# Summing the first modulation vectors over rows on VectorE instead of the matrix engine, in a two-block transformer kernel

## The chip, the core and the metric

The kernel runs on one core of a Trainium2 chip. A core has engines with a queue of instructions each: TensorE (PE, matrix multiply; its weight loads are listed as PEld), VectorE (DVE), ScalarE (ACT), GpSimd (POOL) and SyncE (SP), which here issues the DMAs. The metric is the device time of one execution in microseconds; lower is better.

## The reference, cut to what matters

Two blocks run one after the other on x of 256 rows by 1024 columns, all in fp32. The first is a mixer of four branches, a layer norm, a mixture of 16 experts and a second layer norm. The second is two layers of three sublayers; each sublayer is modulated by vectors made from a condition c:

```python
cond = jax.nn.silu(c)                       # 1024 numbers
for i in range(DEPTH_2):                    # 2 layers
    mod = cond @ ada_w[i] + ada_b[i]        # 1024 x 9216 weights per layer
    sh0, sc0, g0, sh1, sc1, g1, sh2, sc2, g2 = jnp.split(mod, N_MOD, axis=-1)
    h = modulate(rmsnorm(x, pre_norm[i, 0]), sh0, sc0)
    ...
```

The change is about sh0, sc0 and g0 of layer 0, three vectors of 1024 numbers: each is cond times a 1024 x 1024 block of ada_w. They depend on c alone and can be made at any time before the second block; the kernel makes them in the mixer.

## The kernel before

**Weights.** All weights come as slabs of 1 MB in the order of a plan (class `Weights`). A slab lands in a raw buffer (`raw`, three of them in the mixer; later also `rex`, `wex`, `wey`, `wez`, `wea` and `b4`, which the trace calls b). A slab of kind "split" is then split for the matmuls into a high and a low part: ScalarE writes `whi` (L125) and VectorE `wlo` (L126), in 8 pieces of 128x256. A projection does three matmuls per piece (L276 to L278: high by high, low by high, high by low). `pump` issues the next transfer when a buffer comes free, and splits one slab ahead.

**Modulation.** A slab of kind "ada" holds 256 rows of a block of `ada_w` (two chunks of 128 rows, 1024 columns). Twelve of them make the three vectors of layer 0, sublayer 0: four per vector. The plan interleaves them with the mixer's weights. When the plan comes to one, `side` (L2117) is called. For these twelve the flag `vec` is off: `rowsum` (L2146) multiplies each chunk by its column of cond on TensorE, four matmuls of 128x256 that write rows 0, 32, 64 and 96 of one PSUM tile (`adacc`) over eight chunks. With `vec` on, as for most later vectors, VectorE keeps a running sum `asum` of 128x1024 (L2138 for the first chunk, L2140 for the other seven), and only at the end a `rowsum` with a column of ones sums it over the 128 partitions.

**Draining.** When the next "ada" slab comes, or at the mixer's end, `drain` (L2151) copies `adacc` to `aev` (VectorE, L2160) and writes it out in four small DMAs to `arow` (L2163). `finish` (L2166) adds the bias (`ab`, L2173) later.

**The mixer.** Its projections (`psmm`) fill TensorE's queue. Between them lie the serial parts of the branches: the triangular solve of the delta rule, with `TT` and `mt` on VectorE and `psgdn` and `psgla` on TensorE (L767 to L779), the stick-breaking attention, the gated linear attention, and the merges (`mg`, `macc`, L1103 to L1106). At its end `macc` is split to `xTh` and `xTl` and the output projection (`y`) begins in PSUM banks that the mixer has held until then. The experts' matmuls are `pg`, `pu` and `pd` (L1395).

**Order.** The code is written in the order of the computation. A scheduler sets the order in each engine's queue from the dependences, the buffers and this order; `behind` only says that an instruction comes after given ones. Queues run in order.

Of the kernel before, what the change touches and what calls it, by code (L numbers as in the profile page):

```python
# [198 lines left out]
def interleave(main, side, a, b):  # L199
    out, n = [], 0  # L200
    for i, m in enumerate(main):
        out.append(m)
        while n < len(side) and i + 1 > a + (b - a) * n / len(side):
            out.append(side[n])
            n += 1
    return out + side[n:]
# [251 lines left out]
def mixer_slabs(w_in, w_branch, w_out):  # L458
    w = w_in
    out = []  # L460
    def seg(a, b):
        for c in range(a, b, 256):
            out.append(cols_slab(w, c, c + 256))
    seg(1024, 1536)
    kind, parts, n, c = out[0]
    (_, src), = parts
    out[0] = kind, [((h, h + 4, 0, c), src[:, h:h + 4]) for h in (0, 4)], n, c
    out.append(("split", [((0, KC, 0, 16), w.rearrange("(k p) n -> p k n", p=P)[:, :, 5640:5656]),
                          ((0, KC, 16, 24), w.rearrange("(k p) n -> p k n", p=P)[:, :, 2048:2056])], KC, 24))
    for nm, s in FILL:  # L470
        c = {"q": 512, "v": 1536, "s": 2568}[nm] + 256 * s
        seg(c, c + 256)
    merge = lambda n: mslabs(w, w_branch, n)
    seg(3592, 4104)
    seg(0, 512)
    out += merge(2) + merge(0)
    seg(4616, 5128)
    seg(4104, 4616)
    seg(5128, 5640)
    seg(2056, 2568)  # L480
    out += merge(1)
    seg(5656, 6168)
    out += merge(3)
    for r in range(0, D, 256):
        out.append(rows_slab(w_out, r, r + 256))
    return out
# [712 lines left out]
def moe_slabs(wg, wu, wd):  # L1199
    out = []  # L1200
    raw = lambda w, r: ("raw",) + rows_slab(w, r, r + 1 * RB * P)[1:]
    for q in range(0, E, 2):
        for r in range(0, D, RB * P):
            for w in (wg, wu):
                out += [raw(w[e], r) for e in (q, q + 1)]
        for r in range(0, FE, 2 * P):
            out += [("raw",) + rows_slab(wd[e], r, r + 2 * P)[1:] for e in (q, q + 1)]
    return out


def router_consts(k, a):
    nc, cp = k.nc, k.consts
    wr = cp.tile([P, KC, 2 * E], F32, name="wr")
    nc.gpsimd.memset(wr, 0.0)
    nc.sync.dma_start(out=wr[:, :, 0:E], in_=a["w_router"].rearrange("(k p) e -> p k e", p=P))
    rb = cp.tile([P, 1, E], F32, name="rb")
    nc.sync.dma_start(out=rb[:, 0], in_=bcast(a["router_bias"], E))
    it = cp.tile([P, CAP], F32, name="it")
    nc.gpsimd.iota(it, pattern=[[1, CAP]], base=0, channel_multiplier=0, allow_small_or_imprecise_dtypes=True)
    k.router = wr, rb, it  # L1220


def router_bias(k, bcol, psum_tile):
    nc = k.nc
    pb = psum_tile([P, E])
    for kc in range(KC):
        nc.tensor.matmul(pb, bcol[:, kc:kc + 1].to_broadcast([P, P]), k.router[0][:, kc, 0:E], start=kc == 0, stop=kc == KC - 1)
    k.lnw = k.consts.tile([P, E], F32, name="lnw")
    nc.vector.tensor_copy(k.lnw, pb)
# [511 lines left out]
def load_pos(k, pool, positions):  # L1741
    nc = k.nc
    pi = pool.tile([P, 2], I32, name="rp_i")
    v = bass.AP(tensor=positions.tensor, offset=positions.offset, ap=[[1, P], [P, 2]])
    if positions.dtype == I32:
        nc.sync.dma_start(out=pi, in_=v)
    else:
        p64 = pool.tile([P, 2], positions.dtype, name="rp_64")
        nc.sync.dma_start(out=p64, in_=v)
        nc.vector.tensor_copy(pi, p64.bitcast(I32).rearrange("p (t w) -> p t w", w=2)[:, :, 0])  # L1750
    return pi
# [559 lines left out]
def tile_kernel(ctx, tc, a, out):  # L2311
    nc = tc.nc
    e = ctx.enter_context
    k = Kern(tc)
# [7 lines left out]
    A = k.A = Ada(k, a)  # L2322
    k.W.side = A.side
    k.ops = Ops(nc, tc, k.consts, k.small)
    ms = mixer_slabs(a["w_in"][0], a["w_branch"][0], a["w_out"][0])
    k.W.plan(interleave(ms[:-4], A.slabs(0, 0, False), 4, len(ms) - 6) + ms[-4:])
    k.W.plan(moe_slabs(a["w_gate"][0], a["w_up"][0], a["w_down"][0]))
    k.W.plan(second_slabs(a, A))
    new_x = lambda: k.act.tile([P, 2, D], F32, name="x", tag="x", bufs=1)
# [21 lines left out]

    k.more_slots = more_slots
    with ExitStack() as c:
        m = Mixer(k, c, a, x, xTh, xTl)
        A.setup(adp, dram, lambda s: m.ps.tile(s, F32, name="adps", tag="gdn", bufs=2))
        A.acc_tile(m.ps.tile([P, 512], F32, name="adacc", tag="adacc", bufs=1))
        pos = []

        def later():
            pos.append(load_pos(k, adp, a["positions_2"]))  # L2360
            A.load(m.bp)
            router_consts(k, a)

        def then():
            A.params()
            router_bias(k, A.ln1b, A.psum_tile)

        m.run(later, then)
        k.W.bufs["b4"] = 4
        k.W.side_some(99)  # L2370
        A.drain()
# [75 lines left out]


# [12 lines left out]
```

## Time and profile before

| | |
|---|---|
| median of 3 runs | 1732.62 us (1730.42 to 1734.5) |
| the profiled execution | 1734.04 us, its span 1732.3 us, mean granted clock 0.989 |
| busy TensorE, VectorE, ScalarE, GpSimd | 1676.4, 1122.9, 836.2, 28.3 us |
| read from HBM | 401.11 MB, 232 GB/s over the span |
| chain that ended last | TensorE 51%, VectorE 6%, ScalarE 2%, DMA 1% |

The mixer lasts to about 415 us, the first layer norm and the router to 456 us, the experts to 686 us; then come the second layer norm and the second block. Times in rows are from the span's start. In a row of the stretches each engine has its busy time and, in brackets, its instructions.

### The profile page before, as it was taken

What the parts mean: (1) busy time and instruction counts of PE and PEld (TensorE: products, weight loads), DVE (VectorE), ACT (ScalarE), POOL (GpSimd) and SP (SyncE); (2) the same over time, 40 slices, a digit from 0 to 9 for tenths busy, and PEclk for the clock granted to TensorE, in tenths of its full rate; (3) what the DMA queues carried; (4) which work ended last, traced back from release to release, by engine and by line L of the source; (5) the groups of instructions that cost most, each with busy time, mean ns of one, the idle gap of its engine ahead of it and who ended that gap; (6) DMA issues with size and microseconds to landing.
All of it is one profiled execution on the core that took longest, in us unless ns stands there. A gap on an engine that the chain in (4) does not pass through costs nothing.

```text
span 1732.3 us, 30933 instructions
## 1 busy us (share of the span) xinstructions
PE 1676.4 (97%) x11786; PEld 1412.0 (82%) x11786; DVE 1122.9 (65%) x3100; ACT 836.2 (48%) x2367; POOL 28.3 (2%) x61
## 2 busy tenths in 40 slices
PE   7999999999899997999999999999999999999998
PEld 6998999998534443899878599988999778889986
DVE  5776676666521112888859788895977576786563
ACT  5446594344211111555644755563655475656552
POOL 1000011010000000000000000000000000000000
PEclk9999999999999999899999999999999999999999
DMA  6334657459999996599834659893988656347550
GB/s 209 122 122 147 194 177 236 149 182 353 353 390 395 395 392 251 174 308 302 318 107 149 245 189 312 288 346 118 325 259 274 223 188 218 130 145 250 174 204 25
DMA packets 247267, 404.35 MB, mean 233 GB/s; under 512 B 16271, under 2 KB 167478, under 8 KB 247110
## 3 DMA queue, kind: packets, MB, share of 16 engines
q1 hardware_dynamic: 247110, 402.29, 67.6%
q8 instruction: 95, 1.56, 0.4%
q14 instruction: 62, 0.51, 0.1%
HBM read 401.11 MB, written 1.07 MB: 232 GB/s over the span
## 4 chain that ended last, share of the span: by engine, by line
PE 51%; DVE 6%; ACT 2%; DMA 1%; issue 1%; DVEq 0%; ACTq 0%
PE y L276 5%; PE y L278 5%; PE y L277 5%; PE psg L276 4%; PE psg L277 4%; PE psg L278 4%; PE psu L276 4%; PE psu L278 4%; PE psu L277 4%; PE y L1596 2%; PE pj L277 1%; PE adacc L2148 1%; PE pj L276 1%; PE pj L278 1%; DVE wlo L126 1%; ACT scr L288 1%
## 5 line engine op out<-in xcount | busy, mean ns | idle before, releaser
L125 ACT ACTIVATE whi<-raw 128x256 fp32r<-128x256 f32 (+1 forms) x1005 | 330.0, 406 | 231.8 <-PE psmm L277 68.0
L126 DVE TENSOR_TENSOR wlo<-raw,whi 128x256 fp32r<-128x256 f32 (+1 forms) x1005 | 368.6, 425 | 103.6 <-ACT whi L125 103.2
L276 PE MATMUL psmm<-xTh,whi 128*128 128x256 f32 x584 | 170.6, 292 | 7.0 <-DVE gdn_k L592 5.1
L277 PE MATMUL psmm<-xTl,whi 128*128 128x256 f32 x584 | 167.6, 287 | 0.0
L278 PE MATMUL psmm<-xTh,wlo 128*128 128x256 f32 x584 | 167.4, 287 | 0.0
L276 PE MATMUL psg<-xTh,whi 128*128 128x256 f32 x560 | 159.0, 284 | 0.0
L278 PE MATMUL psg<-xTh,wlo 128*128 128x256 f32 x560 | 158.4, 283 | 0.0
L277 PE MATMUL psg<-xTl,whi 128*128 128x256 f32 x560 | 158.4, 283 | 0.0
L126 DVE TENSOR_TENSOR wlo<-rex,whi 128x256 fp32r<-128x256 f32 x296 | 104.1, 417 | 28.9 <-ACT whi L125 28.5
L125 ACT ACTIVATE whi<-rex 128x256 fp32r<-128x256 f32 x296 | 97.1, 405 | 52.9 <-PE y L278 15.4
L276 PEld LDWEIGHTS psmm<-xTh,whi 128*128 128x128 f32 x584 | 112.1, 192 | 12.0 <-ACT whi L125 7.2
L278 PEld LDWEIGHTS psmm<-xTh,wlo 128*128 128x128 f32 x584 | 112.1, 192 | 0.6
L277 PEld LDWEIGHTS psmm<-xTl,whi 128*128 128x128 f32 x584 | 112.1, 192 | 0.5
L276 PE MATMUL psu<-xTh,whi 128*128 128x256 f32 x392 | 111.0, 283 | 0.0
L277 PE MATMUL psu<-xTl,whi 128*128 128x256 f32 x392 | 110.9, 283 | 0.0
L278 PE MATMUL psu<-xTh,wlo 128*128 128x256 f32 x392 | 110.9, 283 | 0.0
L276 PEld LDWEIGHTS psg<-xTh,whi 128*128 128x128 f32 x560 | 107.4, 192 | 1.3 <-issue 1.3
L277 PEld LDWEIGHTS psg<-xTl,whi 128*128 128x128 f32 x560 | 107.4, 192 | 0.0
L278 PEld LDWEIGHTS psg<-xTh,wlo 128*128 128x128 f32 x560 | 107.4, 192 | 0.0
L276 PE MATMUL y<-whi,hh 128*128 128x512 f32 x264 | 105.5, 400 | 0.0
L278 PE MATMUL y<-whi,hl 128*128 128x512 f32 x264 | 104.5, 396 | 0.0
L277 PE MATMUL y<-wlo,hh 128*128 128x512 f32 x264 | 104.4, 395 | 0.0
(696 smaller groups left out, 4057.0 us busy)
## 6 DMA issues: line engine op xcount, KB each, us to landing
raw<-in_ada_w_dram SPq DMA_DIRECT2D x60, 1024.0 KB
raw<-in_w_in_dram SPq DMA_DIRECT2D x39, 1024.0 KB
raw<-in_ffn_w_up_dram SPq DMA_DIRECT2D x33, 1024.0 KB
raw<-in_ffn_w_down_dram SPq DMA_DIRECT2D x28, 1024.0 KB
raw<-in_ffn_w_gate_dram SPq DMA_DIRECT2D x27, 1024.0 KB
rex<-in_ffn_w_gate_dram SPq DMA_DIRECT2D x13, 1024.0 KB
rex<-in_ada_w_dram SPq DMA_DIRECT2D x12, 1024.0 KB
rex<-in_ffn_w_down_dram SPq DMA_DIRECT2D x12, 1024.0 KB
```

Source lines behind the costliest of these rows:

```text
L125: nc.scalar.activation(hi[:, c0:c1], t[:, c0:c1], AF.Copy)
L126: nc.vector.tensor_tensor(lo[:, c0:c1], t[:, c0:c1], hi[:, c0:c1].bitcast(F32), op=OP.subtract)
L276: nc.tensor.matmul(out, lh, rh, start=start, stop=False)
L277: nc.tensor.matmul(out, lh, rl, start=False, stop=False)
L278: nc.tensor.matmul(out, ll, rh, start=False, stop=stop)
L288: k.nc.scalar.activation(scr[:, HALVES[j]], v, AF.Square, scale=(RS / D) ** 0.5, accum_out=ss[:, j:j + 1])
L1596: nc.tensor.matmul(ps[c][:, i], raw[i][:, kc, c * P:(c + 1) * P], xT.f[:, kc, ts], start=kc == 0, stop=kc == KC - 1)
L2148: self.k.nc.tensor.matmul(self.acc[32 * c:32 * c + 1], col, v[:, c * T:(c + 1) * T], start=start, stop=stop, tile_position=(0, 32 * c))
```

## The change

The twelve slabs of layer 0, sublayer 0 get `vec` on. Their chunks are then scaled and added by VectorE, and each of the three vectors needs one sum over partitions by TensorE. `asum` needs 4 KB per partition for as long as the mixer runs: a pool for it is opened, and the scratch that the framework holds for DMAs issued by software is set from 16 KB to 1 KB per partition. Most buffers of the kernel so lie some 11 to 15 KB lower in the memory than before.

```diff
-    k.W.plan(interleave(ms[:-4], A.slabs(0, 0, False), 4, len(ms) - 6) + ms[-4:])
+    k.W.plan(interleave(ms[:-4], A.slabs(0, 0, True), 4, len(ms) - 6) + ms[-4:])
...
     with ExitStack() as c:
+        k.hp = c.enter_context(tc.tile_pool(name="adasum", bufs=1))
         m = Mixer(k, c, a, x, xTh, xTl)
...
-    nc = bacc.Bacc("TRN2", target_bir_lowering=False, num_devices=1)
+    nc = bacc.Bacc("TRN2", target_bir_lowering=False, num_devices=1, dynamic_dma_scratch_size=1024)
```

On TensorE the twelve groups of `adacc<-raw` leave the mixer's queue, and three groups of `adacc<-asum,ones` come in (the first in two pairs). How the queues change is shown at three places.

VectorE, in the triangular solve some 70 us from the start, before (`lnw` is a small copy, `TT` and `mt` are the solve, `wlo` a weight split):

```order
L1229 COPY lnw<-adps 128x16
L773 TENSOR_TENSOR TT_562<-TT_562,psgla 128x512
L126 TENSOR_TENSOR wlo<-raw,whi 128x256 x4
L769 TENSOR_TENSOR mt<-psgdn,lev 128x512
L126 TENSOR_TENSOR wlo<-raw,whi 128x256 x4
L773 TENSOR_TENSOR TT_586<-TT_586,psgdn 128x512
L769 TENSOR_TENSOR mt<-psgla,lev 128x512
```

The same place on VectorE now:

```order
L1229 COPY lnw<-adps 128x16
L2138 TENSOR_SCALAR asum<-raw,cond 128x1024
L773 TENSOR_TENSOR TT_565<-TT_565,psgla 128x512
L2140 SCALAR_TENSOR_TENSOR asum<-raw,cond,asum 128x1024
L769 TENSOR_TENSOR mt<-psgdn,lev 128x512
L126 TENSOR_TENSOR wlo<-raw,whi 128x256 x4
L773 TENSOR_TENSOR TT_589<-TT_589,psgdn 128x512
L769 TENSOR_TENSOR mt<-psgla,lev 128x512
L126 TENSOR_TENSOR wlo<-raw,whi 128x256 x4
L773 TENSOR_TENSOR TT_565<-TT_565,psgla 128x512
L2140 SCALAR_TENSOR_TENSOR asum<-raw,cond,asum 128x1024
L769 TENSOR_TENSOR mt<-psgdn,lev 128x512
```

The first additions stand between the steps of the solve.

TensorE at the mixer's end, a piece of the difference (`psmm` of `y3` is the last merge, `y` the output projection):

```order
 L277 MATMUL psmm<-y3l,whi 128x256
 L278 MATMUL psmm<-y3h,wlo 128x256
+L2148 MATMUL adacc<-asum,ones 1x256 x4
 L276 MATMUL y<-whi,xTh 128x512
 L277 MATMUL y<-wlo,xTh 128x512
```

The last sum over partitions stands between the last merge and the output projection.

VectorE at the mixer's end before, from the last `mg` on:

```order
L1105 SCALAR_TENSOR_TENSOR mg<-mg,psmm 128x512
L126 TENSOR_TENSOR wlo<-raw,whi 128x256
L1106 TENSOR_TENSOR macc_2007<-macc_2007,mg 128x512
L126 TENSOR_TENSOR wlo<-raw,whi 128x256 x3
L1144 TENSOR_TENSOR xTl<-macc_2007,xTh 128x512
L126 TENSOR_TENSOR wlo<-raw,whi 128x256 x12
L2173 TENSOR_TENSOR ab<-ab,arow 24x128
```

And now:

```order
L1105 SCALAR_TENSOR_TENSOR mg<-mg,psmm 128x512
L2160 COPY aev<-adacc 128x256
L1106 TENSOR_TENSOR macc_1993<-macc_1993,mg 128x512
L1248 MEMSET rt_gs 128x16
L126 TENSOR_TENSOR wlo<-raw,whi 128x256 x3
L1144 TENSOR_TENSOR xTl<-macc_1993,xTh 128x512
L126 TENSOR_TENSOR wlo<-raw,whi 128x256 x5
L2173 TENSOR_TENSOR ab<-ab,arow 24x128
L126 TENSOR_TENSOR wlo<-raw,whi 128x256 x8
```

The last copy `aev` stands where a split stood, and `ab` comes eight splits earlier against the layer norm behind it.

SyncE early in the mixer, a piece of the difference (`wez` is a buffer for expert weights, `ab` a bias):

```order
 L109 DMA raw<-in_w_in_dram 128x8x256 x2
-L2128 DMA ab<-in_ada_b_dram 24x128 x3
+L2128 DMA ab<-in_ada_b_dram 24x128
+L109 DMA wez<-in_w_down_dram 128x2x1024
+L2128 DMA ab<-in_ada_b_dram 24x128 x2
 L109 DMA raw<-in_w_in_dram 128x8x256
 L109 DMA raw<-in_ada_w_dram 128x2x1024
```

One slab of expert weights comes at the mixer's beginning instead of behind its end, since its place in memory (188384 to 196576 of each partition) overlapped before with buffers that the mixer's branches use and now lies above them.

## Rows read from the trace of the kernel before

**Rows 1.** The page: its span, and busy time, share and instructions of each engine.

```profile
span 1732.3 us, 30933 instructions
...
PE 1676.4 (97%) x11786; PEld 1412.0 (82%) x11786; DVE 1122.9 (65%) x3100; ACT 836.2 (48%) x2367; POOL 28.3 (2%) x61
```

**Rows 2.** Stretch 60 to 415 us: length, busy time per engine, clock, DMA share, GB/s.

```profile
60.00:415.00 355.00, 351.31 (x2938) 330.51 (x2937) 239.22 (x596) 191.57 (x478) 20.42 (x18) 1.00 0.55 182
```

**Rows 3.** Waits of PE, 60 to 415 us: total, times, longest (first of four).

```profile
PE psgla L1033 <- ACT zs L1027: 1.4, 1, 1.4
```

**Rows 4.** Timeline of PE around one slab: start, length, instruction.

```profile
200.35 0.28 PE L277 MATMUL psmm<-xTl,whi 128*128 128x256 f32 x1
200.47 0.28 PE L278 MATMUL psmm<-xTh,wlo 128*128 128x256 f32 x1
200.68 1.04 PE L2148 MATMUL adacc<-raw,cond 128*1 128x256 f32 x16
...
201.99 0.28 PE L278 MATMUL psmm<-xTh,wlo 128*128 128x256 f32 x1
```

**Rows 5.** Stretches of the experts, their start, and what lies before.

```profile
466.00:676.00 210.00, 206.21 (x980) 87.38 (x978) 30.30 (x65) 25.10 (x48) 0.00 (x0) 0.99 1.04 392
456.00:466.00 10.00, 10.00 (x55) 4.49 (x56) 2.24 (x9) 1.03 (x3) 0.00 (x0) 1.00 0.83 290
380.00:456.00 76.00, 70.95 (x501) 62.71 (x502) 55.36 (x186) 33.83 (x85) 4.50 (x7) 0.96 0.93 342
```

**Rows 6.** adacc alone, 60 to 415 us: PE, PEld, DVE busy; its instructions.

```profile
60.00:415.00 355.00, 14.29 (x192) 3.94 (x192) 1.26 (x3) 1.00 0.55 182
...
L2160 DVE COPY aev<-adacc x3: 417/418/425, 178.1 to 384.6; 128x256 f32<-128x256 f32 x3
```

**Rows 7.** Timeline of PE around one later sum of asum.

```profile
756.55 0.28 PE L278 MATMUL psg<-xTh,wlo 128*128 128x256 f32 x1
...
757.65 0.28 PE L278 MATMUL psu<-xTh,wex 128*128 128x256 f32 x1
```

**Rows 8.** Timelines of DVE and PE at the mixer's end.

```profile
414.24 0.68 DVE L1105 SCALAR_TENSOR_TENSOR mg<-mg,psmm 128x512 f32<-128x512 f32 x1
414.84 0.42 DVE L126 TENSOR_TENSOR wlo<-raw,whi 128x256 fp32r<-128x256 f32 x1
...
414.98 0.50 PE L276 MATMUL y<-whi,xTh 128*128 128x512 f32 x1 [1.18 <-DVE mg L1105]
```

**Rows 9.** The tile asum, whole span: ns shortest/median/longest, first and last start.

```profile
L2140 DVE SCALAR_TENSOR_TENSOR asum<-raw,cond,asum x63: 1270/1282/1286, 716.9 to 1345.2; 128x1024 f32<-128x1024 f32 x63
...
L2138 DVE TENSOR_SCALAR asum<-raw,cond x7: 742/743/745, 710.9 to 1323.8; 128x1024 f32<-128x1024 f32 x7
```

**Rows 10.** asum alone, 800 to 820 us: PE, PEld, DVE busy.

```profile
800.00:820.00 20.00, 0.00 (x0) 0.00 (x0) 8.95 (x7) 1.00 0.90 283
```

**Rows 11.** The whole of that stretch: PE, PEld, DVE, ACT, POOL.

```profile
800.00:820.00 20.00, 20.00 (x170) 20.00 (x169) 19.16 (x37) 10.47 (x31) 0.00 (x0) 1.00 0.90 283
```

**Rows 12.** Timeline of DVE in the solve, first two of the waits.

```profile
71.63 0.69 DVE L773 TENSOR_TENSOR TT<-TT,psgla 128x512 f32<-128x512 f32 x1 [1.20 <-PE psgla L772]
...
78.95 0.69 DVE L773 TENSOR_TENSOR TT<-TT,psgla 128x512 f32<-128x512 f32 x1 [1.25 <-PE psgla L772]
```

**Rows 13.** Stretch 160 to 170 us, columns as in rows 2.

```profile
160.00:170.00 10.00, 9.09 (x76) 7.53 (x74) 10.00 (x24) 9.48 (x24) 0.00 (x0) 1.00 0.22 65
```

**Rows 14.** Timeline of SP: the last group of arow.

```profile
407.34 5.98 SPq L2163 DMA_DIRECT2D arow<-aev  x4
```

**Rows 15.** Timeline of DVE: the addition ab.

```profile
423.95 0.27 DVE L2173 TENSOR_TENSOR ab<-ab,arow 24x128 f32<-24x128 f32 x1
```

**Rows 16.** The tile wez, 400 to 430 us: its first transfer's issue.

```profile
L109 SPq DMA_DIRECT2D wez<-in_w_down_dram x1: 587/587/587, 420.2 to 420.2; - x1
```

**Rows 17.** Waits of SP, 380 to 470 us: for the first expert.

```profile
SPq L109 <- PE pg L1395: 4.9, 1, 4.9
```

**Rows 18.** The tile wey: the first expert's matmuls.

```profile
L1395 PE MATMUL pg<-wey,xg x8: 592/592/643, 455.9 to 459.0; 128*64 128x512 f32 x8
```

## The prediction

> **What bounds the kernel now.** I read the page's busy table first, then the stretch that the change touches (60 to 415 us, in the mixer), its waits, and the stretches behind it. Over the span TensorE is busy 97%, VectorE 65% [rows 1]. In 60 to 415 us TensorE is busy 351.31 of 355 us, VectorE 239.22, ScalarE 191.57, and the DMA share is 0.55 at a granted clock of 1.00 [rows 2]. TensorE itself has four waits with a named releaser there, the longest of 1.4 us [rows 3]. A projection step starts every 0.12 us, matmul behind matmul [rows 4]. So the mixer lasts as long as TensorE's queue, and a matmul taken out of that queue is worth the time it holds it.
>
> Behind the mixer come the first layer norm and the router, then the mixture of experts. There the DMA share is 1.04 at 392 GB/s from 466 to 676 us [rows 5]: the experts end when their weights have come. From there on TensorE is the bound again, and the change touches nothing.
>
> **What is removed.** Twelve slabs of 1 MB, each with 8 matmuls of one condition column (16 records, since an fp32 matmul here shows as two): 192 records [rows 6]. Their records cover 14.29 us of TensorE [rows 6]. What a slab costs the queue is read from the starts around one: the steps at 200.47 and 201.99 us lie 1.52 us apart, with a slab's 16 records and two further steps between them [rows 4]. Three steps alone would take 3 x 0.12 = 0.36 us, so the slab costs 1.16 us: 12 x 1.16 = 14.0 us.
>
> **What is added on TensorE.** Three sums over partitions, 4 matmuls with a column of ones each. Eleven of these stand in the trace later on. At one the steps before and after start at 756.55 and 757.65 us, 1.10 us for three steps and the sum [rows 7], so it costs 1.10 - 0.36 = 0.74 us; three would cost 2.2 us. The order shows the last of them behind the mixer's last projection step and ahead of the output projection. There TensorE now idles 1.18 us until VectorE's mg is done [rows 8], so that sum hides and 2 x 0.74 = 1.5 us stay. Behind mg the order puts the copy aev, in the place of one weight split of 0.42 us [rows 8]; the copy takes 0.418 us [rows 6]. If the output projection's PSUM bank waits for that copy too, it starts 0.4 us later. I take 1.5 + 0.4 = 1.9 us, with 1.5 and 2.6 as its ends. The first sum is split in two pairs, which I leave within these ends.
>
> **What is added on VectorE.** Each of the three vectors needs one scaling (743 ns) and seven multiply-adds (1282 ns) of 128x1024 [rows 9]: 3 x 0.743 + 21 x 1.282 = 29.2 us. VectorE has 355 - 239 = 116 us free in the stretch, so it goes to about 268 of 355 us, 75%. What of the 29.2 us comes through to TensorE no row of the mixer shows, since VectorE does no such additions there. The lower end is zero. From 800 to 820 us seven of these additions take 8.95 us [rows 10], VectorE is busy 19.16 of 20 us, and TensorE still has 20.00 us and 170 matmuls [rows 11], one every 0.118 us, with the ready-split weights never late. The upper end is all 29.2 us. A gain is excluded: an earlier freed raw slot speeds only transfers, and TensorE waits for none here. The mixer differs from 800 to 820 us in its serial chains. In the triangular solve (TT, mt) VectorE and TensorE take turns: VectorE waits 1.20 to 1.25 us for each TT [rows 12], and the order puts four of the additions between those operations. A 1.28 us addition fits almost exactly into one such gap; where it stands ahead of an operation that is ready, it delays it by up to its length. The projection steps between them in TensorE's queue cover most of that. The nearest row is that of 800 to 820 us, but for the chain I take 2.0 us, the length of one or two additions, out of 29.2 us. Against this stands one row: from 160 to 170 us VectorE is busy 10.00 of 10 us and TensorE falls to 9.09 [rows 13]. The order puts no addition into that piece (the stick-breaking part), so it stays as it is.
>
> **What is moved.** The copies aev and the DMAs arow behind them go later. On SyncE each group of four small DMAs waits for its copy, with weight slabs queued behind. The third now follows the last mg, where before SyncE issued this group from 407.34 us on, over 5.98 us [rows 14]. mg ends at 414.24 + 0.68 us [rows 8], so on this scale the copy ends near 415.3 us and the four are out some 3 us later; behind them stand the layer norm's parameters and further expert slabs, whose slots are soon full anyway (below). VectorE's addition ab needs the last of them to land; it stands before the layer norm at 423.95 us [rows 15], about eight splits earlier in the new order, so at worst it would hold VectorE for 1 to 2 us. I count that within the range.
>
> The smaller DMA scratch and the new pool move addresses, and with them one slab: the order shows the first wez slab (128x2x1024 in fp32, 1.05 MB) early in the mixer, where it was issued at 420.2 us [rows 16]. Its transfer takes 1.05 MB / 392 GB/s = 2.7 us. It hides in the mixer, where the DMA share is 0.55. Whether it shortens the experts depends on what holds their transfers at the start: from 456 to 466 us the share drops to 0.83 [rows 5], since the slots are full, and SyncE waits up to 4.9 us for the first expert's matmul pg to free one [rows 17]. With one slab less to load the slots are only full sooner. I take 0 and keep 2.7 us of gain as the other end.
>
> **Does the gain last?** The experts' transfers run without a pause once the first matmuls free slots, and those start at 455.9 us [rows 18], after a chain of projection, layer norm and router that follows the mixer's end and hardly waits for DMA. So the whole chain, and with it the end of the transfers, moves by what the mixer gains.
>
> **The sum.** -14.0 + 1.9 + 2.0 = -10.1 us. The profiled execution took 1734.0 us (span 1732.3 us [rows 1] and 1.7 around it), 1.4 over the median of 1732.6. Both move alike, so against the median: 1732.6 - 10.1 = 1722.5 us, and 1723.9 us for an execution like the profiled one.
>
> **A rule set against the rows.** The sum counts the time that a slab's matmuls hold TensorE [rows 4]. The same records need only 3.94 us of weight loading [rows 6], against 14.29 us of matmul. The Trainium skill's page "Perfetto Trace Analysis" (Identifying the Most-Contended Engine) holds that matmul busy time is no good measure of headroom and that weight-load busy time should be taken. By that measure the removed slabs are worth 3.9 us and not 14.0, and the sum would be about nothing. The starts in rows 4 speak for 14.0, so I weigh it low, as rival three.
>
> **The rivals.**
> One, slower: VectorE becomes the late one. Its queue runs in order, so each addition ahead of a wlo split, a TT or an mt holds all behind it, and TensorE's queue then stands at the step that needs it. This decides once more than 14.0 - 1.9 = 12.1 us of the 29.2 us come through, 41%. With two thirds, 19.5 us, it is 1732.6 - 12.1 + 19.5 = 1740.0 us. For it: rows 12 and 13. Against: rows 10 and 11, and the 116 us free. Chance 0.12.
> Two, the experts keep their end: if their transfers were held by something that doesn't move with the mixer, the gain goes into a longer wait before them, and the time stays 1732.6 us. For it: share 1.04 for 210 us. Against: 0.83 ahead of that, with slots full and matmuls awaited. Chance 0.08.
> Three, only the weight loads count: 3.94 us less for the slabs, about 0.3 more for three sums (24 loads against 192, and they partly overlap), 2.0 for VectorE: 1732.6 - 1.6 = 1731.0 us. Chance 0.04.
> Four, the early slab does shorten the experts: 1722.5 - 2.7 = 1719.8 us. For it: the share is 0.93 from 380 to 456 us [rows 5], near full. Chance 0.14.
> That the change does less than it says is excluded by the order: all twelve groups of adacc<-raw are gone from the mixer.
>
> **How the numbers follow.** The forecast keeps 0.62, with its own range of 1719 to 1727 us (VectorE's share 0 to 5 us, the other ends above). A measurement of this kernel tells about 0.2%, 3.5 us, from no change: 1729.1 to 1736.1 us. Faster: 0.60 of the forecast and 0.14 = 0.74. Same: 0.02, 0.08 and 0.04 = 0.14. Slower: 0.12. The range goes from 1717 us (rival four with nothing lost on VectorE is 1717.8) to 1733 us (rivals two and three in); rival one and some 0.05 below are left out.
>
> **What will show it.** adacc<-raw gone before 415 us, 24 records of adacc<-asum there; TensorE's waits in the mixer still a few microseconds, with VectorE as releaser for at most 2 us more; the first matmul of the output projection near 405 us where it was 414.98; pg<-wey near 446 us; and the experts' transfers ending about 10 us earlier. Wrong would be: TensorE waiting for wlo, TT or mt by more than 5 us in all (rival one), pg<-wey early but the transfers ending as before (two), the mixer shorter by under 4 us without new waits (three), the interval between pg<-wey and the end of the transfers shorter by 2 to 3 us (four).

## The result, and the profile after

The changed kernel took 1721.77 us (median of five runs, 1719.44 to 1723.54), the kernel before beside it 1730.81 us (1730.12 to 1734.5): a ratio of 0.9941, with an interval of 0.9930 to 0.9952, so 10.2 us less (8.3 to 12.1). The forecast was 1722.5 us, 10.1 us less, and faster. Time and sign came out as forecast. The trace shows that two terms behind them did not: 3.3 us were gained in a place where I had put nothing, and about as much was lost again later.

The page of the changed kernel, its span and the busy table (before: [rows 1]):

```profile
span 1721.8 us, 30619 instructions
...
PE 1659.8 (96%) x11618; PEld 1406.3 (82%) x11618; DVE 1150.5 (67%) x3124; ACT 836.7 (49%) x2367; POOL 28.0 (2%) x61
```

The mixer's stretch, columns as in [rows 2], then the same stretch with the instructions on `adacc` alone (before: [rows 6]; PE, PEld, DVE):

```profile
60.00:405.00 345.00, 340.06 (x2763) 327.58 (x2762) 266.62 (x618) 192.84 (x482) 20.15 (x18) 1.00 0.58 190
...
60.00:405.00 345.00, 2.42 (x24) 0.40 (x24) 1.25 (x3) 1.00 0.58 190
```

The 192 records are gone and 24 stand in their place; VectorE has 27.4 us more (266.62 against 239.22), TensorE is still busy 340 of 345 us. Its waits there, five of seven:

```profile
PE y L276 <- DVE aev L2160: 1.0, 1, 1.0
PE psmm L277 <- DVE y0l L1077: 0.9, 1, 0.9
PE psmm L276 <- DVE a_xc L592: 0.8, 1, 0.8
PE psgla L1033 <- ACT zs L1027: 0.8, 1, 0.8
PE psmm L276 <- ACT mg L1088: 0.4, 1, 0.4
```

Before there were four, [rows 3] and these. None is for the branch output `y0` (`y0h`, `y0l`):

```profile
PE y L276 <- DVE mg L1105: 1.2, 1, 1.2
PE psgdn L857 <- DVE onr L271: 0.6, 1, 0.6
PE psmm L276 <- DVE a_xc L592: 0.4, 1, 0.4
```

To see where the time went, take the start of one and the same instruction in both traces and subtract. The order of the projection's and merges' matmuls (`psmm`) is the same in all kernels here, but for one merge where a run changes it and a few filling matmuls that a run adds, so the n-th of them can be followed. Timeline of TensorE in the changed kernel, two of them and the first matmul of the output projection (before: 57.17, 401.98 and 414.98 us):

```profile
56.04 0.28 PE L277 MATMUL psmm<-xTl,whi 128*128 128x256 f32 x1
...
390.94 0.28 PE L277 MATMUL psmm<-xTl,whi 128*128 128x256 f32 x1
...
404.27 0.50 PE L276 MATMUL y<-whi,xTh 128*128 128x512 f32 x1 [0.97 <-DVE aev L2160]
```

| start of | before | after | gained so far |
|---|---|---|---|
| a projection matmul ahead of the first slab | 57.17 | 56.04 | 1.1 |
| one in the last merge | 401.98 | 390.94 | 11.0 |
| the output projection | 414.98 | 404.27 | 10.7 |
| the first expert | 455.9 | 445.7 | 10.2 |
| the last `ys<-pd` pair of the experts on ScalarE | 681.75 | 668.21 | 13.5 |
| VectorE behind the branch of L1515 (the `If` on an expert that is too full) | 686.87 | 674.98 | 11.9 |
| end of the span | 1732.3 | 1721.8 | 10.5 |

The first 1.1 us lie ahead of the first slab and are counted to the start of the execution, not to the change. The granted clock differed there (0.83 and 0.91 from 20 to 40 us), but that is not all of it: the second trace of the changed kernel has 0.83 too and is 0.8 us ahead, and over all traces below this lead lies between 0.1 and 3.4 us. The mixer itself gained 11.0 - 1.1 = 9.9 us, the experts 3.3 us, and 3.0 us were lost behind them.

### The profile page after: what moved, and what is told of

Same layout as the page of the kernel before. It is cut to its first block, busy times and chain, and to the rows that moved or that the text cites. A ratio compares the mean times of both kernels' runs of the same rounds, so it can differ in the third digit from the quotient of the medians.

```text
span 1721.8 us, 30619 instructions
## 1 busy us (share of the span) xinstructions
PE 1659.8 (96%) x11618; PEld 1406.3 (82%) x11618; DVE 1150.5 (67%) x3124; ACT 836.7 (49%) x2367; POOL 28.0 (2%) x61
## 3 DMA queue, kind: packets, MB, share of 16 engines
HBM read 401.11 MB, written 1.07 MB: 234 GB/s over the span
## 4 chain that ended last, share of the span: by engine, by line
PE 50%; DVE 6%; ACT 3%; DMA 1%; issue 1%; DVEq 0%; ACTq 0%
PE y L276 5%; PE y L278 5%; PE y L277 5%; PE psg L276 4%; PE psg L277 4%; PE psg L278 4%; PE psu L276 4%; PE psu L278 4%; PE psu L277 4%; PE y L1596 2%; PE pj L277 1%; PE pj L276 1%; PE pj L278 1%; PE adacc L2148 1%; DVE wlo L126 1%; ACT scr L288 1%
## 5 line engine op out<-in xcount | busy, mean ns | idle before, releaser
L2140 DVE SCALAR_TENSOR_TENSOR asum<-raw,cond,asum 128x1024 f32<-128x1024 f32 x84 | 107.5, 1280 | 5.8 <-DMA raw<-in_ada_w_dram 4.7
```

Source lines behind the costliest of these rows:

```text
L2140: nc.vector.scalar_tensor_tensor(self.sum, raw[:, q], cond, self.sum, op0=OP.mult, op1=OP.add)
```

## The experiments

Two questions had to be told apart. What do the terms of the mixer measure, and does VectorE's new work cost TensorE anything (theory V) or do the slabs' matmuls, now gone, leave other waits open that they had covered (theory C)? And are the 3.3 us of the experts due to the early slab (theory A), and what was lost later to chance or to the change (theory B)? Each run stands beside its own kernel before, at 1732.5 to 1733.0 us. The table at the end of this section has the starts of all of them.

**The same kernel again.**

> The changed kernel once more, for the spread of its trace. In the first trace the gain was 11.0 us at the end of the mixer, 10.2 us at the first expert's matmul (445.7 us against 455.9), 13.5 us at the end of the last expert's matmuls (ys at 668.2 against 681.8), 11.9 us when VectorE went on behind the branch of line 1515, and 10.5 us at the end. Theory A (mixer and early slab both real, the later losses chance): the first three come again within 0.7 us; VectorE's wait at the branch, 4.9 us against 3.2 before, and the loss of 1.4 us near 1460 us do not come again, so that the gain at the end is 12 to 13.5 us in a run without them. Theory B (the later losses belong to the change): the wait at the branch is again above 4.5 us and 1.4 us is lost again near 1460 us. The time by both is 1719 to 1723 us, a ratio of 0.993 to 0.995.

1723.89 us, ratio 0.9941 (0.9928 to 0.9953). Output projection 405.32, first expert 446.66, experts' end 669.2 us: 9.7, 9.3 and 12.6 us gained, 0.9 to 1.3 us less than in the first trace and so outside the 0.7 us of theory A; 0.4 us of that lies ahead of 57 us. In the wait at the branch the answer is A. VectorE's waits there, in the first trace and in this one (before: 3.2 us):

```profile
DVE x L1170 <- DVEq L1515: 4.9, 1, 4.9
```

```profile
DVE x L1170 <- DVEq L1515: 3.2, 1, 3.2
```

The loss of 1.4 us near 1460 us came again, which was B's sign, and three more such losses with it. The stretches of this trace where they lie (length, PE, clock, DMA share, GB/s):

```profile
900.00:910.00 10.00, 7.77 (x58) 0.83 0.92 319
960.00:970.00 10.00, 9.53 (x62) 0.83 0.51 180
1450.00:1460.00 10.00, 10.00 (x67) 0.83 0.54 179
1490.00:1500.00 10.00, 8.61 (x51) 0.83 0.85 307
```

Each is a few microseconds at the lower clock. The kernel before has one of its own from 1500 to 1510 us (0.83) and 1.00 in these four. Three of the four came in this execution and not in the other of the same kernel, and each moves the end by 1 to 2 us. The one near 1450 us is in eight of the eleven traces with the slabs out of TensorE's queue, and in neither of the two with them there; whether it belongs to the change stays open. The table of starts is therefore read up to the place it is about, and not at the end.

**The two halves of the change.**

```diff
 # scratch_only: the kernel before, and
+    nc = bacc.Bacc("TRN2", ..., dynamic_dma_scratch_size=1024)
 # vec_only: the changed kernel, and
-    nc = bacc.Bacc("TRN2", ..., dynamic_dma_scratch_size=1024)
+    nc = bacc.Bacc("TRN2", ...)
```

> The kernel before with only the DMA scratch set to 1 KB: the addresses move, and the first wez slab is loaded early in the mixer; VectorE and TensorE have the work they had. Theory A (the early slab shortens the experts): the first pg<-wey starts within 1 us of 455.9, but the time from there to the last expert's ys is 222.5 us as in the changed kernel and not 225.9 as before; the time is 2.7 to 3.4 us shorter, a ratio near 0.998. Theory of the prediction (the slab is worth nothing, the slots are only full sooner): the time from pg<-wey to ys stays 225.9 us, ratio 1.000.

> The changed kernel without the smaller DMA scratch: the twelve slabs go to VectorE, and the first wez slab is issued behind the mixer's buffers as before. Theory of the prediction: all of the gain comes from the mixer, 10.1 us, a ratio of 0.9942, and the time from the first pg<-wey to the last ys is the same as in the changed kernel. Theory A: the mixer's end is as early as in the changed kernel (output projection's first matmul at 404 to 405 us), but the time from pg<-wey to ys is back at 225.9 us; the gain is 7 us if the early slab's 3.4 us are taken off the 10.2 us measured, or 10 us if what was lost later was chance.

The scratch alone: 1730.52 us, ratio 0.9989 (0.9980 to 0.9997), 1.9 us less. VectorE's share alone: 1724.82 us, 0.9942 (0.9927 to 0.9958), the whole gain. The pool of 4 KB fits without the smaller scratch. From the first expert to `ys` the two took 222.9 and 223.2 us, where it was 225.8 before and 222.5 with both, but part of that is the clock: before and after have a stretch at 0.83 in it (650 to 660 and 640 to 650 us), these two do not. So neither theory holds: with the slab late (issued at 408.5 us) the experts got shorter as well, and with it early (35.8 us) they did not get 3.3 us shorter.

What shortens them is seen in TensorE's timeline. Of one pair of experts, before:

```profile
547.33 1.02 PE L1395 MATMUL pu<-b,xg 128*64 128x512 f32 x2
...
549.09 0.64 PE L1395 MATMUL pu<-rex,xg 128*64 128x512 f32 x1
549.10 0.64 PE L1395 MATMUL pu<-b,xg 128*64 128x512 f32 x1
...
560.38 1.93 PE L1395 MATMUL pd<-raw,hT 128*64 128x512 f32 x4
...
563.86 3.65 PE L1395 MATMUL pd<-raw,hT 128*64 128x512 f32 x12
```

and in the changed kernel:

```profile
537.09 0.59 PE L1395 MATMUL pu<-b,xg 128*64 128x512 f32 x1
537.10 0.59 PE L1395 MATMUL pu<-rex,xg 128*64 128x512 f32 x1
...
547.52 3.60 PE L1395 MATMUL pd<-raw,hT 128*64 128x512 f32 x16
```

These matmuls use half of the columns (128*64). Two on different halves start 0.01 us apart and take 0.42 us together. In the old order some stand alone, at 0.4 to 0.5 us each: 16 of `pd<-raw` take 1.93 + 3.65 us in two pieces, and 3.60 us in one. It is the order of the queue that changed, for 3.3 us; 1055 records stand in the stretch in both. Counted over it, 36 of 768 half-column records stand alone before (none of the others starts within 0.1 us) and 24 in the changed kernel. Nine of the traces below have the changed kernel's order, and all nine take 222.4 to 222.5 us. The three other runs have orders of their own with 32 alone: 222.9 and 223.2 us in the two halves above, and 224.6 us in `no_rowsums`, which has the stretch at the lower clock. Why the scheduler orders them so only with both halves of the change was not tried.

**VectorE's additions left out, and done twice.**

```diff
 # no_adds                                   # adds_twice
-                else:                       +  nc.vector.scalar_tensor_tensor(self.sum2, raw[:, q],
+                elif name != (0, 0):        +      cond, self.sum, op0=OP.mult, op1=OP.add)
```

> The changed kernel without the 21 multiply-adds on VectorE (the three scalings and the sums over partitions stay), so that 26.9 us of VectorE work are left out and with them 7/8 of each of the three vectors. It measures what of VectorE's work comes through to TensorE. Theory of the prediction: 2 us, so that the output projection starts at 402 to 403 us and the time is about 2 us below the changed kernel's. Rival (VectorE the late one): 5 us and more below. Other rival (VectorE's work hides wholly): output projection at 404 to 404.5 us and the same time as the changed kernel, within 1 us.

> The changed kernel with each of the 21 multiply-adds done twice (the second result goes to a tile that nothing reads): 26.9 us more of VectorE work in the mixer, about 294 of 345 us busy. Theory V, VectorE's work comes through in proportion: the 2 to 3 us that the additions cost come once more, output projection at 406 to 407 us, time 2 to 3 us above the changed kernel's; by rival one (two thirds) 18 us. Theory C, the additions themselves hide: output projection within 1 us of the changed kernel's, and the same time within 1 us.

Without the additions 1719.63 us, 0.9924 (0.9912 to 0.9937); twice 1723.96 us, 0.9954 (0.9940 to 0.9967). From 57 us to the last merge they gain 12.9 and 7.0 us, where the changed kernel gains 9.9: 3.0 and 2.9 us for 26.9 us of additions, a ninth. That looks like theory V in proportion. But up to 211 us, with the triangular solve behind, the three had gained the same within 0.5 us (5.4, 5.8 and 5.7). All of the difference arises from 222 us on, and the first part of it, 1.2 and 2.0 us at 248 us, at the merge of y0. There, in the changed kernel:

```profile
223.71 0.50 PE L276 MATMUL psmm<-y0h,whi 128*128 128x256 f32 x2 [0.35 <-ACT y0h L1076]
225.08 0.38 PE L277 MATMUL psmm<-y0l,whi 128*128 128x256 f32 x1 [0.87 <-DVE y0l L1077]
...
225.46 0.42 PE L276 MATMUL psmm<-y0h,whi 128*128 128x256 f32 x1
225.68 0.41 PE L277 MATMUL psmm<-y0l,whi 128*128 128x256 f32 x1
```

TensorE waits 0.35 and 0.87 us for the end of that branch's serial chain (a scan, then y0h on ScalarE, then y0l on VectorE). Behind it its matmuls start 0.21 us apart and not 0.12: the granted clock is 0.50, the lower of its two levels (1.2 GHz), for 15 matmuls, which costs 15 x 0.09 = 1.4 us.

Without the additions the second sum over partitions is ready earlier, and its 8 records stand just there:

```profile
224.63 0.59 PE L2148 MATMUL adacc<-asum,ones 128*1 128x256 f32 x2
...
225.58 0.60 PE L2148 MATMUL adacc<-asum,ones 128*1 128x256 f32 x6
226.45 0.38 PE L277 MATMUL psmm<-y0l,whi 128*128 128x256 f32 x1 [0.26 <-DVE y0l L1077]
```

They fill most of the wait, and the clock stays at 1.00. So what `no_adds` gains here it gains by the place of a sum. In the changed kernel that sum stands at 285 us and holds TensorE 0.6 us, another part of the 3.0 us.

A third part is the additions' own. In the changed kernel:

```profile
232.00 2.59 DVE L2140 SCALAR_TENSOR_TENSOR asum<-raw,cond,asum 128x1024 f32<-128x1024 f32 x2
...
245.10 1.06 ACT L918 ACTIVATE l_e<-l_d 128x1024 f32<-128x1024 f32 x1 [0.63 <-DVE l_d L916]
...
247.01 0.39 PE L276 MATMUL psmm<-y0h,whi 128*128 128x256 f32 x1 [0.39 <-ACT mg L1088]
...
250.42 0.38 PE L276 MATMUL psmm<-xTh,whi 128*128 128x256 f32 x1 [0.34 <-DVE mg L1105]
```

Two additions hold VectorE ahead of the chain of the gated linear attention. ScalarE then waits for `l_d`, copies `mg` later, and TensorE waits for `mg`. One or both of these waits of TensorE stand in every trace with the additions. They stand in none of the four without: the kernel before, `scratch_only`, `no_adds` and, below, `no_rowsums`. From 253 to 260 us (times of the kernel before) the changed kernel loses 1.3 us of its gain, `no_adds` 0.4 and `no_rowsums` 0.2. This is theory V, for about 1 us.

**The slabs off TensorE with nothing put on VectorE.**

```diff
 # no_rowsums: the kernel before, and
-                if not vec:
+                if name == (0, 0):
+                    if kc == 0:
+                        self.rowsum(cond, raw[:, q], True, True)
+                elif not vec:
```

> The kernel before with 21 of the 24 chunks of the first three modulation vectors left out of the sum on TensorE (24 of 192 records stay; the vectors are wrong by the rest), and nothing put on VectorE, with the scratch and the addresses of before. It separates the price of the slabs from VectorE. Theory C (the slabs covered the scalar and vector chain of the branch y0, and taking them out is what opens the stall): TensorE waits for y0h and y0l near 224 us also here, by 0.8 us or more, the clock falls behind it, and the output projection starts 9.5 to 10.5 us earlier than in the kernel before (404.5 to 405.5 us). Theory V (the additions on VectorE make the stall): no wait there, and the output projection starts 168/16 x 1.07 = 11.2 us and the share that the last sums no longer take, 11 to 12.5 us, earlier (402.5 to 404 us), as without the additions.

1720.39 us, 0.9933 (0.9920 to 0.9946). TensorE's waits in its mixer:

```profile
PE psmm L276 <- DVE a_xc L592: 1.3, 1, 1.3
...
PE psmm L277 <- DVE y0l L1077: 0.9, 1, 0.9
```

and its stretch from 226 us, columns as in [rows 2]:

```profile
226.00:228.00 2.00, 2.00 (x12) 2.00 (x11) 1.32 (x4) 1.97 (x6) 0.00 (x0) 0.50 0.74 187
```

The same wait and the same half clock, with no addition on VectorE. From 227 to 237 us it loses 1.8 us of its gain, the changed kernel 2.0. So the wait at y0 is theory C: the slabs had covered it. From 57 us to the last merge it gains 9.75 us, like the changed kernel, with the same number of `adacc` records. That the two agree is in part chance: up to 211 us it gains 1.7 us less, behind that 1.5 us more. (Its output projection, at 401.86 us, lay beyond V's range, since 3.4 us of it came from ahead of 57 us; counted from there it is 9.7 us and C's.) Doing the additions twice does add there: the wait for y0h grows to 1.3 us.

**The merge of y0.**

```diff
 # cut; merge_order, first piece of the merge
-                        mm3(nc, ps[:, j], wh.., wl.., y[0][:, c], y[1][:, c], c == 0, c == 3)
+                    for c in range(4):
+                        nc.tensor.matmul(ps[:, j], wh.., y[0][:, c], start=c == 0, stop=False)
+                        nc.tensor.matmul(ps[:, j], wl.., y[0][:, c], start=False, stop=False)
+                    for c in range(4):
+                        nc.tensor.matmul(ps[:, j], wh.., y[1][:, c], start=False, stop=c == 3)
 # fill and merge_fill: ahead of the piece
+                if not (n or hh or s):
+                    k.warm(6, ps[:, 0, 0:P])      # 4 in merge_fill
```

> The changed kernel with one other order of TensorE's matmuls: in the first piece of the merge of y0, the eight matmuls that need only y0h go ahead of the four that need y0l. In the changed kernel TensorE waits there 0.35 us for y0h and 0.87 us for y0l (225.1 us), and for 2.9 us behind that its matmuls are spaced 0.21 us instead of 0.12 (granted clock 0.50 in 226 to 228 us); the kernel before has neither. Theory C (cover): the slabs' matmuls had covered the serial chain of that branch, TensorE now catches up with it, and the stall and the lower clock behind it are the cost. Then the wait for y0l falls to below 0.4 us, the clock stays at 1.00 in 224 to 230 us, the output projection starts 1.5 to 2.3 us earlier (402 to 403 us in a trace that is like the first) and the time is 1.5 to 2.3 us below the changed kernel's. Theory V (VectorE itself is late because of the additions): the wait moves to a later place, and the output projection starts where it did, 404 to 405 us.

> The changed kernel with six matmuls more on TensorE (identity by identity, 128x128, overwritten at once) ahead of the merge of y0, some 1.5 us of work that nobody needs, so that TensorE arrives there later and does not run dry at y0h and y0l. If the lower clock behind that place follows from the stall (theory S), the granted clock in 224 to 232 us stays 1.00, the waits of 0.35 and 0.87 us are gone, and the 15 matmuls spaced 0.21 us are at 0.12: 1.5 us more work, 1.2 us less waiting and 1.4 us less at half clock, so the output projection starts about 1 us earlier in spite of more work. If the clock falls there for another reason, the output projection starts 0.3 us or more later than in the changed kernel. The time moves by 1 us or less either way, so that the trace decides.

> The changed kernel with the other order in the merge of y0 and four of those matmuls ahead of it. Theory S: no stall is left in the merge of y0, the clock stays at 1.00 there, and the output projection starts 1.5 to 2 us earlier than in the changed kernel; time 1 to 2 us below it, the fastest of the versions with the mixer's slabs on VectorE. Otherwise it is like the run with the other order alone, 404.3 us for the output projection.

The other order: 1720.58 us, 0.9932 (0.9919 to 0.9945). The wait for y0l is gone, but one of 0.46 us for y0h stays, the clock is low behind it as before, and 1.1 us of waiting comes up at 247 us, where it was 0.4: 0.4 us gained at the last merge of the 1.5 to 2.3 expected: what is gained at y0 (1.1 us more at 248 us) is mostly lost again at the place of the waits for `mg`. With the six filling matmuls: 1718.88 us, 0.9930 (0.9915 to 0.9946). No wait is left at y0, and the clock falls all the same (from 224 us on, in this trace):

```profile
222.00:224.00 2.00, 2.00 (x10) 1.47 (x11) 2.00 (x5) 2.00 (x8) 0.00 (x0) 1.00 0.00 0
224.00:226.00 2.00, 2.00 (x12) 2.00 (x11) 2.00 (x7) 1.97 (x7) 0.00 (x0) 0.50 0.22 40
```

So theory S falls: the trace shows TensorE busy without a gap ahead of the drop. What sets the clock there stays open. With both: 1718.70 us, 0.9925 (0.9912 to 0.9937), no wait and a clock of 1.00 at y0, 10.8 us gained at the last merge, 0.9 more than the changed kernel where 1.5 to 2 were expected; 1.2 us of waiting for `mg` stay. By its median it is the fastest of the versions that compute all, by 2.8 us against the changed kernel by the two ratios; the intervals overlap, so that is not shown, and only 0.9 us of it come from the mixer. The rest lies between output projection and first expert, which took 39.3 us here and 38.5 in `fill`, against 41.4: there the clock is at its lower level for some 7 us in the traces of the changed kernel, 3 in that of `merge_fill` and not at all in that of `fill`. It is not at all in `adds_twice` either (38.5), so this doesn't go with the merge; what decides it was not tested.

**The rest of the modulation on VectorE.**

```diff
-    ada = {n: A.slabs(*n, n[1] < 2) for n in ((0, 1), (0, 2), (1, 0), (1, 1), (1, 2))}
+    ada = {n: A.slabs(*n, True) for n in ((0, 1), (0, 2), (1, 0), (1, 1), (1, 2))}
 # cut: and a pool for asum in each of the two blocks
```

> The changed kernel with the 16 modulation slabs that are still summed on TensorE (8 in the sparse attention and 8 in the differential attention of the second block) summed by VectorE too, in a running sum of its own for the second block: it tests whether the price holds elsewhere. By the same sum: 16 slabs at 1.07 us off TensorE, 4 sums at 0.74 us on, -17.1 + 3.0 = -14 us at most, a time near 1708 us. Theory C (a matmul is worth its time only where TensorE's queue is the bound, and in these two parts it waits for softmax and sorting): half of that or less, 1714 to 1720 us. Theory V: VectorE's 20.5 us per eight slabs lie ahead of the attention's own VectorE work, no gain, 1720 us or above.

> Both together: all modulation slabs on VectorE and the other order in the merge of y0. Theory C: the two gains add, since they lie in different blocks: 1.5 to 2.3 us below the run with all slabs on VectorE. Theory V: no difference to that run.

1735.44 us, 1.0015 (1.0006 to 1.0024), and with the other order 1733.59 us, 1.0008 (0.9999 to 1.0018): slower than with the mixer's twelve alone by some 13 us, on theory V's side and further than I had reckoned with. Between the two lie 1.9 us by the medians and 0.4 us at the last merge, so C's 1.5 to 2.3 us did not come. By the starts 9.3 us are lost in the sparse attention and 6.3 in the differential one. The two stretches in the changed kernel, columns as in [rows 2]:

```profile
893.00:987.00 94.00, 88.26 (x663) 64.34 (x661) 81.17 (x292) 56.72 (x180) 0.00 (x0) 1.00 0.59 201
...
1390.00:1515.00 125.00, 117.87 (x922) 102.02 (x921) 88.74 (x304) 76.76 (x266) 0.00 (x0) 0.99 0.61 203
```

with all slabs on VectorE:

```profile
893.00:996.00 103.00, 84.50 (x554) 65.31 (x553) 97.43 (x306) 56.67 (x179) 0.00 (x0) 0.90 0.53 176
...
1399.00:1530.00 131.00, 115.84 (x809) 105.65 (x809) 107.30 (x320) 77.69 (x266) 0.00 (x0) 0.92 0.58 193
```

and the longest of TensorE's waits in the latter, in each:

```profile
PE ppt L1921 <- DVE sm L1916: 7.4, 2, 4.1
...
PE dot L2041 <- DVE dO L2037: 5.2, 2, 5.0
```

VectorE was busy 81 of 94 and 89 of 125 us there. With the additions TensorE waits for its softmax (`sm`) and for `dO`, and the clock falls to 0.90 and 0.92 on average. In the second VectorE had time left, but it is waited for in turn, step by step. This is rival one, in another place.

The starts, from the traces. "Gain" is the shift of a projection matmul against the kernel before, less its shift at 57.17 us; the matmuls start there at 211.51, 247.98 and 401.98 us. The last two columns are from the output projection to the first expert, and from there to the last `ys`. Each kernel has one trace, the changed one two, and these differ by 0.7 us in the second and third column: less than that between two kernels shows nothing.

| | gain at 211 | at 248 | at 402 | y to pg | pg to ys |
|---|---|---|---|---|---|
| before | | | | 41.0 | 225.8 |
| changed | 5.7 | 4.9 | 9.9 | 41.4 | 222.5 |
| changed, again | 5.7 | 4.2 | 9.2 | 41.3 | 222.5 |
| scratch_only | -0.1 | -0.1 | 0.6 | 41.0 | 222.9 |
| vec_only | 5.6 | 4.7 | 9.9 | 42.1 | 223.2 |
| no_adds | 5.4 | 6.1 | 12.9 | 39.4 | 222.5 |
| adds_twice | 5.8 | 2.9 | 7.0 | 38.5 | 222.5 |
| no_rowsums | 4.0 | 3.4 | 9.7 | 41.0 | 224.6 |
| merge_order | 5.7 | 6.0 | 10.3 | 41.0 | 222.4 |
| fill | 5.7 | 4.6 | 9.6 | 38.5 | 222.5 |
| merge_fill | 5.7 | 6.1 | 10.8 | 39.3 | 222.5 |
| all_vec | 5.7 | 4.2 | 9.3 | 41.2 | 222.5 |
| all_vec_merge | 5.7 | 5.4 | 9.7 | 41.4 | 222.5 |

## Why the prediction was right, and where it was not

**The mixer is bound by TensorE.** Held. The gain was 9.9 us by the last merge and 9.6 at the output projection (10.7 - 1.1), where the sum said 10.1. That it came so near is in part luck: the parts below miss in both directions.

**The slabs, 14.0 us.** Right in kind, a little too large. Of one slab, TensorE before and after:

```profile
356.04 0.97 PE L963 MATMUL psgla<-l_qi,l_S 128*128 128x32 f32 x8
356.94 1.04 PE L2148 MATMUL adacc<-raw,cond 128*1 128x256 f32 x16
357.91 0.38 PE L276 MATMUL psmm<-y1h,whi 128*128 128x256 f32 x1
```

```profile
347.16 0.97 PE L963 MATMUL psgla<-l_qi,l_S 128*128 128x32 f32 x8
347.96 0.37 PE L276 MATMUL psmm<-y1h,whi 128*128 128x256 f32 x1
```

From 356.04 to 357.91 are 1.87 us, from 347.16 to 347.96 0.80: 1.07 us for this slab, where I had read 1.16 from one place [rows 4]. Twelve at 1.07 are 12.8 us, where twelve at 1.16 are 13.9 and were written down as 14.0. Rival three is out: in the mixer the weight loads' busy time fell by 2.9 us (330.51 to 327.58) and the time by 9.9, so here the matmuls' starts were the measure. The Trainium skill's "Perfetto Trace Analysis" (Identifying the Most-Contended Engine) gives weight-load busy time as a measure of TensorE's headroom; taken as the price of a matmul with a single column of weights, the trace does not agree with it (2.9 against 12.8 us).

**The sums, 0.74 us each.** About right. The one at 285.17 us lies between projection starts at 284.96 and 285.71, 0.75 - 0.12 = 0.63 us. The first came in two pairs, and a pair costs nearly as much as a whole one: the second of them lies between starts at 194.08 and 194.81 us, 0.73 - 0.12 = 0.61 us. The last is hidden, and the output projection waits for the copy `aev` (0.97 us) where it waited for `mg` (1.18): 0.3 us lost from the last merge to it, against 0.4 taken.

**VectorE, 2.0 us in the solve's chain.** Wrong in its place. In the solve nothing was lost: up to 211 us the changed kernel gained 5.7 us, and without the multiply-adds 4.0 (`no_rowsums`) and 5.4 (`no_adds`). Five slabs at 1.07 less the first sum explain some 4.2 of the 5.7; where the rest comes from was not tested. What was lost came at two places behind it. At the merge of y0 it is 1.2 us of waiting and 1.4 us of lower clock, a net 2.0 us of the gain, and there the run with no VectorE work shows nearly the same. At the waits for `mg` it is about 1 us, and that is the additions'. The step that failed is the search for the place: I looked at where the first additions stand, and not at which serial chain the removed matmuls had been covering, nor at the additions ahead of the gated linear attention. What the additions cost in all can't be given as one number, since each kernel has its own order: nothing against `no_rowsums`, 3.0 us against `no_adds` (part of it the place of a sum), 2.9 us more when doubled. All lie within the 0 to 5 us of the forecast's own range, and far below rival one's 12.1 us.

**The late copies and the DMAs behind them.** SyncE now waits 9.4 us there, and issues the last group of `arow` at 404.24 us, when the last copy has ended (403.80 + 0.41), with weight slabs behind it. From 405 to 415 us the DMA share is 0.72, and TensorE is busy 10.00 of 10: no cost, as counted.

**The experts end when their weights have come.** Wrong. TensorE's waits from the first expert to the last, in the changed kernel, are all that it names, and the kernel before has the same:

```profile
PE pht L1421 <- DVE h L1418: 2.1, 2, 1.1
PE adps L2194 <- DVE gp L2183: 1.1, 1, 1.1
PE pd L1395 <- ACT hT L1425: 0.5, 1, 0.5
```

No wait for a transfer. The row that I had read for a DMA share of 1.04 also has TensorE busy 206.21 of 210 us [rows 5]: both were full, and TensorE set the pace. That the gain lasts was right, for another reason (the whole of TensorE's queue moves), so rival two was out from the start.

**Rival four** gave its sign, an interval shorter by 3.3 us, where I had announced 2 to 3; but its mechanism, the slab loaded early, is not the cause. The order of half-column matmuls is.

**The sum.** 9.6 us at the output projection, 0.5 lost in layer norm and router, 3.3 gained in the experts, 3.0 lost behind them (1.7 at the branch, which did not come again in the next execution, the rest mostly at the lower clock), and 1.1 from the start: 10.5 us between the two profiled executions. That the median fell within 0.7 us of the forecast is owed in part to a gain and losses that happened to cancel.

## What to carry to other kernels

Work moved from a full engine to a freer one is worth what the trace shows between the starts around it, here 1.07 us for 16 records, as long as the engine that takes it has room: in the mixer, with VectorE busy 67% and projection matmuls to cover it, it paid 9.9 of 12.8 us, the new sums included; in the attentions, with VectorE busy 86% and 71% and TensorE waiting for it in turn, the same edit lost some 13 us. The busy share alone does not tell the two apart (67% and 71%); who waits for whom does. Before taking work out of a full queue, look for the serial chains that end beside it and ask what covers them when it is gone. And where two resources are both full, the waits of the engine say which of them sets the pace, not the shares.

## What the runs showed that I had not expected

Matmuls that use 64 columns run two at a time when those next to each other in the queue use different halves (starts 0.01 us apart, 0.42 us for both), and one at a time otherwise; the order alone was worth 3.3 us. The Trainium skill's "TensorE: Matmul & The Clock Gate" (Part 3: Packing small matmuls) says that matmuls that fill only part of the array can be placed on different tiles of it and then run at the same time, and the trace agrees.

The granted clock fell to 0.50 for some 3 us at one place of the mixer, at 224 to 226 us, in nine of the eleven traces with the slabs out of TensorE's queue and in neither of the two with them, also where the trace shows no gap of TensorE ahead of it. The two without the fall are `no_adds` and `merge_fill`, and why those two is open. Elsewhere some such falls come and go between executions of one kernel, 1 to 2 us each, so that a difference of 2 us between two medians of five runs says little without the starts.
